# ScalarE counts the widest block of each search group by signs, the S5 matrix loads move to the SP queue, and a few scale steps to GpSimd

## The chip, the cores and the metric

The kernel runs on one core of a Trainium2 chip. The metric is the device time of one execution in microseconds (us). The engines are named as in the profile: PE is TensorE's matmul (PEld its weight load), DVE is VectorE, ACT is ScalarE, POOL is GpSimd, SP is SyncE, which here only issues DMAs. Each engine takes its instructions in a fixed order and waits at one that is not ready; a DMA is issued from an engine's queue, in the order of that engine.

## The reference

One layer over 1024 positions of width 1024. The input is normalised by its root mean square, scaled and shifted, and multiplied with one wide matrix; the columns of the product feed two mixers and their gates.

```
h = rms_norm(x, norm_g) * (1 + scale) + shift
xa, za, q, k, v, zb, qi, ki, wi, ga, gb = split(h @ w_in)
ya = gelu(s5_mixer(xa, ...)); ... ; ya = (ya * silu(za)) @ w_a_o
yb = dsa_mixer(q, k, v, qi, ki, wi);  yb = (yb * silu(zb)) @ w_b_o
merged = sigmoid(ga) * ya + sigmoid(gb) * yb
return x + gate * (merged @ w_out)
```

`s5_mixer` is a diagonal complex state space recurrence (32 groups of 16 channels, 64 states each). `dsa_mixer` is sparse attention: a small indexer gives each query a score for each earlier key, and the query attends only to the 256 keys of highest score. A final norm follows.

## The kernel before

Tiles are 128 positions, numbered 0 to 7; large products are split into a high and a low part and done as three matmuls of 128x512 (L137 to L139). The Tile framework's scheduler fixes each engine's order at build time from priorities and its own model of time; it also allocates buffers of one tag in the order in which the program names them.

**Norm.** `turn` works on pairs of tiles: ACT sums squares (L229), `rstd_of` (L85 to L96) turns the sums into scales with tiny DVE steps and one square root on ACT, DVE scales `x_sb` (L232), PE transposes (L236).

**Indexer scores** (L464 to L486) leave `score[i]` for tiles 2 to 7, of 128 x 128(i+1) numbers each.

**Search.** For each row the kernel looks for the value that 256 scores exceed, by 12 steps of bisection (L788 to L800). Tiles form two groups, (7, 5, 3) and (6, 4, 2). In each step DVE counts, for each of the three tiles of a group, the scores above the trial value `mid` (function `count`, L764 to L768: one pass with a running sum), ACT makes a sign of the three counts (`side`, L797), and ACT moves three `mid`s (L799). So there are 72 counts on DVE.

**Finalisation** (L801 to L818), tile by tile in the order 7, 5, 3, 6, 4, 2: one more count (`cj..._h`, written to the one buffer of tag "cj"), `j` (L812), the eight largest (L813), two tiny steps, a match and replace (L816), the mask (L817), and on ACT the additive `bias` of the attention (L818). The tile `j` has tag "cf" with two buffers; `gsum` (L722), a sum over eight loaded blocks `wg`, is named earlier under the same tag. Then DVE tests that all counts fit (`good`, `sound`, L822 to L824), PE sums the verdict over partitions (`flag_ps`, L826), and a branch (L830) takes a slow exact search if the test fails. PE's own row for the flag stands in its order after the matmuls of the gates and ahead of the attention's first (`l`, L891).

**S5** runs in eight blocks (q, L583 to L682). For a block GpSimd builds `mt` and `en` (L600 to L610), PE makes the kernel `k_ps` (L620), ACT copies it to `k` (L624), GpSimd adds a diagonal (L629), and eight small DMAs on ACT's queue spread it into the matrix `mk` (L632, two buffers). PE makes states (`s_ps`), ACT copies them (`sp`, L642), DVE rotates and scans them (L654 to L665) to `hs` (L670, L671), and PE adds the two products `u,mk` (L675) and `hs,en` (L677) to `y_ps`; ACT applies the activation (L680).

**Filling work.** Beside S5 PE runs the gate columns GA (eight blocks of 128 columns, 48 dense matmuls each, `gates`, L710 to L718), then GB 0 and 1 and ZB 0 to 3; each half block is evicted by ACT (L715), ZB's then also by DVE (L717). The other GB and ZA blocks fill the attention. The weights come by SP's queue (`load_w`, L108 to L115, two buffers), and are split by a cast on ACT and a subtraction on DVE (L77, L78).

Of the kernel before, what the change touches and what calls it, by code (L numbers as in the profile page):

```python
# [11 lines left out]
BF = mybir.dt.bfloat16  # L12
I32 = mybir.dt.int32
AF = mybir.ActivationFunctionType
OP = mybir.AluOpType
# [4 lines left out]
D = 1024  # L20
L = 1024
# [3 lines left out]
TOPK = 256  # L25
EPS = 1e-6
# [8 lines left out]
def tile_hybrid(ctx, tc, x, c, norm_g, w_mod, b_mod, w_in, a_re, a_im, b_re, b_im,  # L35
                c_re, c_im, d_skip, log_dt, w_glu, b_glu, w_a_o, w_b_o, w_out,
                final_g, out):
    nc = tc.nc
# [17 lines left out]
    def bank(name):  # L56
        return ps1.tile([128, 512], F32, name=name, tag="b1")
# [15 lines left out]
    def staged(name, dtype=F32, shape=(128, L)):  # L73
        return stage.tile(list(shape), dtype, name=name, tag="sg")
# [7 lines left out]
        tc.add_manual_dep(later.ins, earlier.ins.name, mybir.DependencyInfo(  # L82
            mybir.DependencyClass.NoSync, mybir.DependencyReason.DATA), reason="order")

    def rstd_of(t, n=1):  # L85
        a, b, y, r = (t[:, i * n:(i + 1) * n] for i in range(4))
        nc.vector.tensor_scalar(a, a, 1.0 / D, EPS, op0=OP.mult, op1=OP.add)
        nc.scalar.sqrt(b, a)
        nc.vector.reciprocal(y, b)
        if n == 1:  # L90
            nc.vector.scalar_tensor_tensor(b, y, a, y, op0=OP.mult, op1=OP.mult)
        else:
            nc.vector.tensor_mul(b, y, y)
            nc.vector.tensor_mul(b, b, a)
        nc.vector.tensor_scalar(b, b, -0.5, 1.5, op0=OP.mult, op1=OP.add)
        nc.vector.tensor_mul(r, y, b)  # L96
        return r
# [63 lines left out]
    T = 8  # L161
# [11 lines left out]
    with ExitStack() as st:  # L173
# [49 lines left out]
        def turn(half):  # L223

            for t2 in range(4 * half, 4 * half + 4, 2):
                stat = p0.tile([128, 8], F32, name=f"st{t2}", tag="st", bufs=4)
                for t in (t2, t2 + 1):
                    junk = p0.tile([128, D], BF, name=f"junk{t}", tag="junk", bufs=1)
                    nc.scalar.activation(junk, x_sb[t], AF.Square, accum_out=stat[:, t - t2:t - t2 + 1])  # L229
                rstd = rstd_of(stat, 2)  # L230
                for t in (t2, t2 + 1):
                    nc.vector.tensor_scalar_mul(x_sb[t], x_sb[t], rstd[:, t - t2:t - t2 + 1])  # L232
            for k in range(ND):
                ps = bank(f"xt{half}_{k}")
                for j in range(4):
                    nc.tensor.transpose(ps[:, 128 * j:128 * j + 128],  # L236
                                        x_sb[4 * half + j][:, 128 * k:128 * k + 128], ident)
                (nc.scalar.copy if k in ((0, 1, 3, 5, 7), (0, 1, 2, 3, 4, 5, 6, 7))[half] else nc.vector.tensor_copy)(
                    xT[k][:, 512 * half:512 * half + 512], ps)

        turn(0)
        h_hi, h_lo = parts(ND, "h")
        mp = bank("mod_ps")
# [29 lines left out]

        modulation(0)
        turn(1)
        modulation(1)
        qps = [[dense_bank(f"qi{m}_ps") if 2 * m + j < 3 else bank(f"qi{m}_ps") for j in range(2)]
               for m in range(3)]
        for dt in range(ND):
# [3 lines left out]
            scale, bias = ab[dt][:, 1:2], ab[dt][:, 0:1]  # L283

            for sl in [slice(512 * j, 512 * j + 512) for j in range(2)] if dt < 2 else [slice(0, L)]:
# [3 lines left out]
                for m in range(3):  # L289
                    a = slice(128 * m, 128 * m + 128)  # L290
                    for j in range(sl.start // 512, sl.stop // 512):
                        b = slice(512 * j, 512 * j + 512)
# [37 lines left out]
    score, bias = {}, {}  # L330
# [7 lines left out]
    sepool = search.enter_context(tc.tile_pool(name="sepool", bufs=1, side="right"))  # L338
    leads = []
    with ExitStack() as st:  # L340
# [23 lines left out]
        for e in range(2):  # L364
            a = slice(64 * e, 64 * e + 64)
# [98 lines left out]
        for i in groups[0] + groups[1]:  # L464
            w = 128 * (i + 1)
            for h in range(8):
                for o, n in chunks(w):
# [5 lines left out]
                    r = p1.tile([128, 512], F32, name=f"r{i}_{h}_{o}", tag="r", bufs=3)  # L473
# [4 lines left out]
                    else:  # L478
                        nc.vector.scalar_tensor_tensor(dst, r[:, :n], wi_t[:, i, h:h + 1], dst,  # L479
                                                       op0=OP.mult, op1=OP.add)  # L480
# [102 lines left out]
    for m in range(4):  # L583
# [3 lines left out]
        for half in range(2):  # L587
# [35 lines left out]
            ks_ = p2.tile([16, 4, T, 16], F32, name=f"k{q}", tag="kk", bufs=1)  # L623
# [5 lines left out]
            nc.gpsimd.tensor_add(ks_[:, :, 0], ks_[:, :, 0], dg)  # L629
            mk = mks[q % 2]  # L630
            for s in range(T):
                nc.scalar.dma_start(mk[s::8, :, s:], ks_[:, :, 0:T - s])  # L632

            ps = bank(f"s{q}_ps")
            for g in range(4):
# [10 lines left out]
            cj, sj = ct[:, jr], sn_t[:, jr]  # L646
# [3 lines left out]
            for ri in range(2):  # L650
# [11 lines left out]
                                         op0=OP.mult, op1=OP.add)  # L662
# [5 lines left out]
            for e in range(2):  # L668
                a = slice(64 * e, 64 * e + 64)
# [25 lines left out]
    t = staged("vraw")  # L695
# [27 lines left out]
    for kt in range(ND):  # L723
        t = staged(f"wg{kt}")
# [5 lines left out]
    b = staged("bgate")[0:1]  # L730
# [30 lines left out]
    def scr(name, dtype=F32, n=6):  # L761
        return sepool.tile([128, n], dtype, name=name)

    def count(src, at, op, dst, name, dtype=BF):  # L764
        w = src.shape[1]
        j = sepool.tile([128, L], dtype, name=name, tag="cj", bufs=1)[:, :w]
        nc.vector.tensor_scalar(j, src, at, None, op0=op, op1=OP.add, accum_out=dst)  # L767
        return j  # L768
# [4 lines left out]
    half = scr("half", n=STEPS + 2)  # L773
    for n in range(STEPS + 2):
        nc.gpsimd.memset(half[:, n:n + 1], 0.5 ** n)
    below, ranks = scr("below", n=1), scr("ranks", n=8)
    nc.gpsimd.memset(below, 0.5 - TOPK)
    for n in range(8):
        nc.gpsimd.memset(ranks[:, n:n + 1], float(TOPK - 1 - n))
    cgt = scr("cgt")  # L780
    best = sepool.tile([128, 12, 8], F32, name="best")
    step = sepool.tile([128, 6, STEPS + 2], F32, name="step")
    nc.vector.tensor_sub(most, most, least)
# [2 lines left out]
    mids, sides = ([[sepool.tile([128, 3], F32, name=f"{n}{g}", tag=f"{n}{g}", bufs=2)  # L786
                     for _ in range(STEPS + 1)] for g in range(2)] for n in ("mid", "side"))
    for g, tiles in enumerate(groups):  # L788
        for n, i in enumerate(tiles):
            nc.scalar.activation(mids[g][0][:, n:n + 1], least[:, i - 2:i - 1], AF.Identity,  # L790
                                 bias=step[:, i - 2, 1:2])
    for b in range(STEPS):
        for g, tiles in enumerate(groups):
            cnt = sepool.tile([128, 3], F32, name=f"cnt{g}_{b}", tag=f"cnt{g}", bufs=2)
            for n, i in enumerate(tiles):
                count(score[i], mids[g][b][:, n:n + 1], OP.is_gt, cnt[:, n:n + 1], f"cj{i}_{b}")
            nc.scalar.activation(sides[g][b], cnt, AF.Sign, bias=below)  # L797
            for n, i in enumerate(tiles):
                nc.scalar.activation(mids[g][b + 1][:, n:n + 1], sides[g][b][:, n:n + 1], AF.Identity,  # L799
                                     scale=step[:, i - 2, b + 2:b + 3], bias=mids[g][b][:, n:n + 1])  # L800
    for g, tiles in enumerate(groups):  # L801
        for n, i in enumerate(tiles):
            e = slice(i - 2, i - 1)
            nc.scalar.activation(sides[g][STEPS][:, n:n + 1], mids[g][STEPS][:, n:n + 1], AF.Identity,
                                 bias=step[:, i - 2, STEPS + 1:])
# [24 lines left out]
    with tc.If(found < 6 * 128):  # L830
# [4 lines left out]
        thr, d, cnt, need = scr("thr", I32), scr("d", I32), scr("cntb"), scr("need")  # L835
# [196 lines left out]
    for k, (m, pieces) in enumerate(steps):  # L1032
# [8 lines left out]
        t = wpool.tile([128, D], F32, name=f"wo{k}", tag="wraw")  # L1041
# [7 lines left out]
    for t in range(NT):  # L1049
        tok = slice(128 * t, 128 * t + 128)  # L1050
        xr, y = xy[:, t % 2], xy[:, 2 + t % 2]
        nc.sync.dma_start(xr, x[tok])
        stat = const.tile([128, 8], F32, name=f"fs{t}", tag="fs", bufs=2)

        pieces = [(0, 512), (512, 512)] if t < NT - 1 else [(0, 512), (512, 256), (768, 256)]
        for n, (o, w) in enumerate(pieces):
            sl = slice(o, o + w)
            ps = pso.tile([128, 512], F32, name=f"o{t}_ps", tag="o")
            for kt in range(ND):
                three(ps[:, :w], m_hi[kt][:, tok], m_lo[kt][:, tok], wo_h[kt][:, sl], wo_l[kt][:, sl],  # L1060
                      kt == 0, kt == ND - 1)
            nc.vector.tensor_mul(y[:, sl], ps[:, :w], gate[:, sl])
            nc.vector.tensor_add(y[:, sl], y[:, sl], xr[:, sl])
            nc.scalar.activation(xr[:, sl], y[:, sl], AF.Square, accum_out=stat[:, 4 + n:5 + n])
        nc.vector.tensor_add(stat[:, 0:1], stat[:, 4:5], stat[:, 5:6])
        if t < NT - 1:
            rstd = rstd_of(stat)
            nc.vector.scalar_tensor_tensor(y, y, rstd, fg, op0=OP.mult, op1=OP.mult)
            nc.sync.dma_start(out[tok], y)
        else:  # L1070
            a, b = slice(0, 512), slice(512, 1024)
            nc.gpsimd.tensor_mul(y[:, a], y[:, a], fg[:, a])
            nc.vector.tensor_add(stat[:, 0:1], stat[:, 0:1], stat[:, 6:7])
            rstd = rstd_of(stat)
            nc.scalar.activation(y[:, a], y[:, a], AF.Copy, scale=rstd)
            nc.scalar.dma_start(out[tok, a], y[:, a])
            nc.vector.scalar_tensor_tensor(y[:, b], y[:, b], rstd, fg[:, b], op0=OP.mult, op1=OP.mult)
            nc.sync.dma_start(out[tok, b], y[:, b])
# [28 lines left out]
```

## Time and profile before

| | |
|---|---|
| time, median of 3 runs | 905.83 us (901.27 to 908.48) |
| the profiled execution | 904.93 us, its span 903.2 us |
| busy over the span | PE 854.9 us (95%), DVE 655.7 (73%), ACT 406.5 (45%), POOL 138.4 (15%) |
| mean granted clock of TensorE | 0.981 of full speed |
| matmuls | 4105 |
| the 72 counts of the search on DVE | 67.6 us, 939 ns each |

A busy row adds the durations of an engine's instructions. A timeline row gives the start, the length, the engine, the line and the tile, and in brackets how long the engine stood idle before it and what released it. A wait row sums those idle times by instruction and releaser. The granted clock is a share of full speed. The mean time of an instruction includes its fixed part, so that of two that follow each other the second can start before the first's end.

### The profile page before, as it was taken

The page shows a single profiled execution, that of the slowest core. Times are in us where ns is not written, and L with a number is a line of the kernel's source. Part 1 is how long each engine was busy: PE and PEld are TensorE (multiplying, and loading weights), DVE is VectorE, ACT ScalarE, POOL GpSimd, SP SyncE. Part 2 cuts the span into 40 slices and gives each one's busy share as a digit, 9 for nine tenths or more (in the row PEclk, how much of TensorE's full clock was granted, in tenths as well). Part 3 has the DMA queues.
Part 4 walks back from the last instruction along what each step waited for, and adds up shares of the span by engine and source line. Part 5 has one row for each costly group of instructions (what it writes and reads, how often), then busy time and mean ns, then how long its engine had stood idle before and what let it go on. Part 6 is the DMA issues. An engine that isn't in the chain of part 4 may idle for free. (4 is left out here: it accounts for less than half of the span.)

```text
span 903.2 us, 12003 instructions
## 1 busy us (share of the span) xinstructions
PE 854.9 (95%) x4105; PEld 704.1 (78%) x4105; DVE 655.7 (73%) x1381; ACT 406.5 (45%) x803; POOL 138.4 (15%) x244
## 2 busy tenths in 40 slices
PE   4999999998889998999989999999999999999996
PEld 4887788876678876878868888887888888777885
DVE  5674898488999895588236776678987776856753
ACT  7552576344446443322235555448564443432311
POOL 0000100069455944000000000000000000221000
PEclk9799999999899999999999999999999999999999
DMA  9925611363443423473334232235224232644431
GB/s 330 319 66 126 154 49 46 66 178 91 122 113 124 113 78 99 124 279 94 117 107 128 88 97 73 70 106 166 68 64 135 71 94 81 216 143 143 151 129 48
DMA packets 124228, 109.86 MB, mean 122 GB/s; under 512 B 20922, under 2 KB 108034, under 8 KB 124164
## 3 DMA queue, kind: packets, MB, share of 16 engines
q1 hardware_dynamic: 96306, 77.20, 28.3%
q10 hardware_dynamic: 27858, 31.87, 12.2%
q8 instruction: 32, 0.52, 0.3%
q14 instruction: 32, 0.26, 0.1%
HBM read 76.41 MB, written 26.22 MB: 114 GB/s over the span
## 5 line engine op out<-in xcount | busy, mean ns | idle before, releaser
L78 POOL TENSOR_TENSOR wo_l<-wo,wo_h 128x1024 fp32r<-128x1024 f32 x5 | 12.2, 2444 | 451.7 <-ACT wo_h L77 423.2
L767 DVE TENSOR_SCALAR_CACHE_REDUCE cj<-score,mid 128x1024 bf16<-128x1024 f32 (+2 forms) x72 | 67.6, 939 | 14.6 <-ACT mid L790 9.1
L894 DVE CUSTOM_DVE_ANT_0 S<-l,bias 128x384 f32<-128x384 f32 (+5 forms) x96 | 52.4, 554 | 27.1 <-PE l L891 18.5
L905 ACT ACTIVATE S<-S,stt 128x128 f32<-128x128 f32 (+7 forms) x64 | 49.1, 770 | 37.3 <-DVE stt L902 37.1
L77 ACT CAST ph<-pt 128x512 fp32r<-128x512 f32 x72 | 41.3, 585 | 43.2 <-PE pt L916 38.1
L78 DVE TENSOR_TENSOR pl<-pt,ph 128x512 fp32r<-128x512 f32 x72 | 48.9, 687 | 9.2 <-ACT ph L77 8.8
L137 PE MATMUL gb_ps<-h_hi,gb_wh 128*128 128x512 f32 x128 | 52.0, 406 | 2.0 <-ACT gbs L715 2.0
L891 PE MATMUL l<-k_s,qt 128*128 128x384 f32 (+5 forms) x192 | 49.9, 347 | 3.4 <-issue 2.3
L138 PE MATMUL gb_ps<-h_lo,gb_wh 128*128 128x512 f32 x128 | 52.3, 408 | 0.0
L139 PE MATMUL gb_ps<-h_hi,gb_wl 128*128 128x512 f32 x128 | 51.7, 404 | 0.0
L138 PE MATMUL o_ps<-wo_l,m_hi 128*128 128x512 f32 (+1 forms) x136 | 51.2, 378 | 0.0
L139 PE MATMUL o_ps<-wo_h,m_lo 128*128 128x512 f32 (+1 forms) x136 | 51.0, 378 | 0.1
L137 PE MATMUL ga_ps<-h_hi,ga_wh 128*128 128x512 f32 x128 | 50.8, 397 | 0.0
L139 PE MATMUL ga_ps<-h_hi,ga_wl 128*128 128x512 f32 x128 | 50.7, 396 | 0.0
L138 PE MATMUL ga_ps<-h_lo,ga_wh 128*128 128x512 f32 x128 | 50.2, 392 | 0.0
L474 ACT ACTIVATE r<-s 128x512 f32<-128x512 f32 (+3 forms) x80 | 39.8, 525 | 22.8 <-PE s L470 16.8
L137 PE MATMUL o_ps<-wo_h,m_hi 128*128 128x512 f32 (+1 forms) x136 | 49.4, 377 | 0.1
L479 DVE SCALAR_TENSOR_TENSOR score<-r,wi_t,score 128x512 f32<-128x512 f32 (+3 forms) x70 | 42.1, 653 | 7.5 <-ACT r L474 6.6
L916 PE MATMUL pt<-ident,S 128*128 128x128 f32 x288 | 46.3, 273 | 0.4 <-DVE S L909 0.4
L916 PEld LDWEIGHTS pt<-ident,S 128*128 128x128 f32 x288 | 36.6, 140 | 11.3 <-DVE S L909 1.0
L470 PE MATMUL s<-ki_s,qi_s 128*128 128x384 f32 (+3 forms) x160 | 42.2, 356 | 1.4 <-DVE wi_t L463 0.9
L891 PEld LDWEIGHTS l<-k_s,qt 128*128 128x128 f32 x192 | 33.9, 189 | 9.7 <-issue 2.4
(402 smaller groups left out, 2402.5 us busy)
## 6 DMA issues: line engine op xcount, KB each, us to landing
wm<-in_w_mod_dram SPq DMA_DIRECT2D x16, 512.0 KB, 6.3
x_sb<-in_x_dram SPq DMA_DIRECT2D x8, 512.0 KB, 5.5
ga_w<-in_w_in_dram SPq DMA_DIRECT2D x8, 512.0 KB, 4.1
gad<-gas ACTq DMA_DIRECT2D x8, 512.0 KB, 2.6
gb_w<-in_w_in_dram SPq DMA_DIRECT2D x8, 512.0 KB, 4.4
wg<-in_w_mod_dram SPq DMA_DIRECT2D x8, 512.0 KB, 5.2
gbd<-gbs ACTq DMA_DIRECT2D x8, 512.0 KB, 3.2
qt<-qd SPq DMA_DIRECT2D x8, 512.0 KB, 3.9
```

The costliest lines, as they stand in the source:

```text
L77: (hi_eng or nc.scalar.copy)(hi, src)
L78: (lo_eng or nc.vector).tensor_sub(lo, src, f32(hi))
L137: paced(nc.tensor.matmul(ps, wh, rh, start=first, stop=False))
L138: paced(nc.tensor.matmul(ps, wh, rl, start=False, stop=False))
L139: mm = nc.tensor.matmul(ps, wl, rh, start=False, stop=last)
L470: mm = nc.tensor.matmul(ps[:, :n], qs[:, h, 128 * i:128 * i + 128], ks[:, e, o:o + n], start=e == 0, stop=e == 1)
L479: nc.vector.scalar_tensor_tensor(dst, r[:, :n], wi_t[:, i, h:h + 1], dst, op0=OP.mult, op1=OP.add)
L767: nc.vector.tensor_scalar(j, src, at, None, op0=op, op1=OP.add, accum_out=dst)
L891: mm = nc.tensor.matmul(ps[:, :n], qt[:, 4 * e2 + 2 * j + g], ks[:, e, o:o + n], start=e == 0, stop=e == 1)
L894: nc.vector.tensor_tensor_reduce(out=S[:, o:o + n], in0=ps[:, :n], in1=bias[i][:, o:o + n], scale=1.0, scalar=NEG, op0=OP.add, op1=OP.max, ...
L905: nc.scalar.activation(S2[j], S2[j], AF.Exp, scale=0.125, bias=nm[:, j:j + 1], accum_out=sm[:, j:j + 1])
L916: mm = nc.tensor.transpose(ps[:, 128 * j:128 * j + 128], Ss[i, g, j][:, 128 * kb:128 * kb + 128], ident)
```

## The change

There are three edits. First, in each of the 12 steps the widest tile of each group (7 and 6) is counted on ACT: a Sign of `mid - score` with a running sum, its elementwise result thrown into `ca`, a scratch tile of tag "cf". The sum is the number of scores below less the number above, so `side` of that tile is made by an instruction of its own with another bias (`signs`) and scale -1, and the one `side` of three counts becomes two. DVE keeps 48 of the 72 counts. Second, the 64 loads of `mk` are issued from SP and no longer from ACT. Third, for the pairs of the second half of the positions five of `rstd_of`'s steps run on GpSimd.

```diff
-    def rstd_of(t, n=1):
+    def rstd_of(t, n=1, eng=None):
+        if eng is not None:
+            eng.tensor_scalar(a, a, 1.0 / D, EPS, op0=OP.mult, op1=OP.add)
+            nc.scalar.sqrt(b, a)
+            nc.vector.reciprocal(y, b)
+            eng.tensor_mul(b, y, y)
+            eng.tensor_mul(b, b, a)
+            eng.tensor_scalar(b, b, -0.5, 1.5, op0=OP.mult, op1=OP.add)
+            eng.tensor_mul(r, y, b)
+            return r
...
-                rstd = rstd_of(stat, 2)
+                rstd = rstd_of(stat, 2, nc.gpsimd if half else None)
...
-                nc.scalar.dma_start(mk[s::8, :, s:], ks_[:, :, 0:T - s])
+                nc.sync.dma_start(mk[s::8, :, s:], ks_[:, :, 0:T - s])
...
+    signs = {}
+    ca = sepool.tile([128, L], BF, name="ca", tag="cf", bufs=2)
+    for g, i in ((0, 7), (1, 6)):
+        signs[i] = scr(f"signs{i}", n=1)
+        nc.gpsimd.memset(signs[i], 128.0 * (i + 1) + 1 - 2 * TOPK)
...
-                count(score[i], mids[g][b][:, n:n + 1], OP.is_gt, cnt[:, n:n + 1], f"cj{i}_{b}")
-            nc.scalar.activation(sides[g][b], cnt, AF.Sign, bias=below)
+                if n:
+                    count(score[i], mids[g][b][:, n:n + 1], OP.is_gt, cnt[:, n:n + 1], f"cj{i}_{b}")
+                else:
+                    nc.scalar.activation(ca[:, :128 * (i + 1)], score[i], AF.Sign, scale=-1.0, bias=mids[g][b][:, 0:1],
+                                         accum_out=cnt[:, 0:1])
+            nc.scalar.activation(sides[g][b][:, 0:1], cnt[:, 0:1], AF.Sign, scale=-1.0, bias=signs[tiles[0]])
+            nc.scalar.activation(sides[g][b][:, 1:3], cnt[:, 1:3], AF.Sign, bias=below)
```

How the change stands in the engines' orders is shown at three places. The line numbers of the changed kernel are 10 higher from `load_w` on and 21 higher behind the search's steps.

**ACT, the start of the search.** Before, the first step's `side` stands in ACT's order ahead of S5's first copies. Now the first Sign (L815, the line that writes `ca` and `cnt_0`) comes behind nearly all of S5 and the eviction of the first half of GA's last block (the second `gas` here).

```order
L725 ACTIVATE gas_3387<-ga_ps 128x512
L652 COPY sp_2636<-s_ps 64x256 x4
L728 DMA gad<-gas_3387 128x1024
L725 ACTIVATE gas_3447<-ga_ps 128x512
L815 ACTIVATE ca,cnt_0_4024<-score_717,mid_3966 128x1024
L77 CAST v_s<-v_ps 128x8x64
L817 ACTIVATE side_3992<-cnt_0_4024,signs_3958 128x1
L815 ACTIVATE ca,cnt_0_4035<-score_715,mid_3979 128x896
L820 ACTIVATE mid_3967<-side_3992,mid_3966,step 128x1
```

All 24 Signs stand from this place to the next one; before, the 24 `side` rows were spread over S5 and all stood ahead of this place.

**ACT, the end of the search**, in the changed kernel; `zbs_3840` is the block ZB 3, the last of PE's dense work ahead of the flag, and L825 the last move of tile 7's trial value, from which the finalisation counts.

```order
L815 ACTIVATE ca,cnt_11_4277<-score_715,mid_3990 128x896
L818 ACTIVATE side_4003<-cnt_11_4266,below 128x2
L820 ACTIVATE mid_3990<-side_4015,mid_3989,step 128x1 x2
L820 ACTIVATE mid_3978<-side_4003,mid_3977,step 128x1
L817 ACTIVATE side_4016<-cnt_11_4277,signs_3960 128x1
L728 DMA zbd<-zbs_3778 128x1024
L820 ACTIVATE mid_3978<-side_4003,mid_3977,step 128x1 x2
L725 ACTIVATE zbs_3840<-zb_ps 128x512
L825 ACTIVATE side_4004<-mid_3978,step 128x1
```

Before, L825's forerunner (L804) stood within S5; now it stands behind the eviction of ZB 3's first half.

**DVE, the finalisation.** Before, the count `cj_h` of tile 7 stood in the middle of S5 and `j` right behind the first piece of `gsum`, with the rest of both interleaved from there on:

```order
L692 TENSOR_SCALAR bg<-bg 128x4
L78 TENSOR_TENSOR v_s<-v_ps,v_s 128x8x64
L727 TENSOR_SCALAR gsum<-wg_3508,sc 128x1024
L812 SCALAR_TENSOR_TENSOR j_4286<-cj_h,score_717 128x1024
L78 TENSOR_TENSOR gb_wl<-gb_w,gb_wh 128x1024
L729 SCALAR_TENSOR_TENSOR gsum<-wg_3511,sc,gsum 128x1024
```

In the changed kernel the whole of it comes behind the eviction of ZB 3 (the first row here), and the second step's counts come where `j` was:

```order
L727 SCALAR_TENSOR_TENSOR zbs_3840<-zbs_3840,zb_ps 128x512
L777 TENSOR_SCALAR cj_h,cgt<-score_717,side_4004 128x1024
L833 SCALAR_TENSOR_TENSOR j_4291<-cj_h,score_717 128x1024
L835 TENSOR_SCALAR best<-ranks,cgt 128x8
L834 MAX best<-j_4291 128x8
L836 SCALAR_TENSOR_TENSOR best<-best 128x8
L78 TENSOR_TENSOR gb_wl<-gb_w,gb_wh 128x1024
L752 TENSOR_TENSOR bgate<-bgate,gate_3904 1x512
L837 MATCH_REPLACE j_4291<-best,j_4291 128x1024
L727 SCALAR_TENSOR_TENSOR zbs_3840<-zbs_3840,zb_ps 128x512
L752 TENSOR_TENSOR bgate<-bgate,gate_3907 1x512
```

From here to `sound` DVE's order holds the finalisation alone. On SP the eight loads of a block's `mk` now stand between the loads of GA's weights, where eight `ga_w` stood in a row before. On PE the order of the dense work, the flag and the attention is what it was.

## Rows read from the trace of the kernel before

**Rows 1.** What PE waited for, whole span (engine, line, releaser: us in total, times, longest).

```profile
PE y_ps L677 <- DVE hs L671: 7.8, 6, 1.9
PE xt L236 <- DVE x_sb L232: 7.2, 4, 5.3
PE y_ps L675 <- DMA mk<-k: 5.8, 3, 3.6
...
PE k_ps L620 <- POOL en L610: 2.3, 1, 2.3
```

**Rows 2.** Busy us (and instructions) of each engine by stretch, PE's granted clock, DMA share, GB/s.

```profile
225.00:250.00 25.00, 21.37 (x96) 17.85 (x95) 24.64 (x34) 9.03 (x24) 12.70 (x16) 0.86 0.46 119
250.00:275.00 25.00, 22.11 (x104) 18.26 (x103) 22.33 (x40) 13.80 (x31) 11.18 (x13) 0.93 0.47 124
...
381.00:452.00 71.00, 68.97 (x302) 56.00 (x301) 46.79 (x76) 18.10 (x27) 0.00 (x0) 0.98 0.51 163
```

**Rows 3.** Timeline of PE in S5 (start, length, instruction, idle before and releaser).

```profile
241.54 0.77 PE L675 MATMUL y_ps<-u,mk 128*128 128x128 f32 x2 [3.63 <-DMA mk<-k]
...
259.76 0.49 PE L677 MATMUL y_ps<-hs,en 128*128 128x128 f32 x2 [1.95 <-DVE hs L671]
...
261.42 0.80 PE L677 MATMUL y_ps<-hs,en 128*128 128x128 f32 x2 [0.94 <-DVE hs L671]
...
342.55 0.46 PE L677 MATMUL y_ps<-hs,en 128*128 128x128 f32 x2 [1.58 <-DVE hs L671]
```

**Rows 4.** Timeline of PE from the first GB matmul to the flag.

```profile
380.09 0.39 PE L137 MATMUL gb_ps<-h_hi,gb_wh 128*128 128x512 f32 x1
...
451.02 1.88 PE L741 MATMUL gate<-gsum,ones 128*1 128x512 f32 x4
452.73 0.19 PE L826 MATMUL flag_ps<-ones,sound 128*1 128x1 f32 x2
```

**Rows 5.** Timeline of DVE, the finalisation of the search.

```profile
327.06 1.27 DVE L767 TENSOR_SCALAR_CACHE_REDUCE cj_h<-score,side 128x1024 bf16<-128x1024 f32 x1
...
381.01 1.22 DVE L812 SCALAR_TENSOR_TENSOR j<-cj_h,score 128x1024 f32<-128x1024 bf16 x1
...
404.62 0.75 DVE L767 TENSOR_SCALAR_CACHE_REDUCE cj_h<-score,side 128x512 bf16<-128x512 f32 x1 [0.91 <-ACT bias L818]
...
429.05 0.08 DVE L824 DVE_READ_ACCUMULATOR good<-cgt,good 128x1 f32 x1
```

**Rows 6.** DVE by form: two passes over the widest tile in the finalisation (busy, mean ns).

```profile
L813 DVE MAX8 best<-j 128x8 f32<-128x1024 f32 x1 | 1.2, 1220 | 0.0
...
L817 DVE SCALAR_TENSOR_TENSOR cj_h<-j,cj_h 128x1024 bf16<-128x1024 f32 x1 | 1.2, 1215 | 0.0
```

**Rows 7.** ACT by form: wide instructions with a sum, evictions, casts (busy, mean ns).

```profile
L715 ACT ACTIVATE gbs<-gb_ps 128x512 f32<-128x512 f32 x16 | 9.3, 590 | 7.8 <-DVE gsum L729 4.7 <-PE gb_ps L139 2.1 <-DVE best L815 1.0
...
L905 ACT ACTIVATE S<-S,stt 128x1024 f32<-128x1024 f32 x8 | 9.1, 1144 | 2.5 <-DVE stt L902 2.4
...
L77 ACT CAST gb_wh<-gb_w 128x1024 fp32r<-128x1024 f32 x8 | 8.4, 1048 | 17.1 <-PE zb_ps L138 9.3 <-PE gb_ps L138 5.1 <-PE ga_ps L138 2.7
...
L905 ACT ACTIVATE S<-S,stt 128x896 f32<-128x896 f32 x8 | 8.3, 1038 | 2.4 <-DVE stt L902 2.4
```

**Rows 8.** Timeline of ACT, one step of the search late in S5.

```profile
308.72 0.30 ACT L797 ACTIVATE side<-cnt,below 128x3 f32<-128x3 f32 x1
309.05 0.95 ACT L799 ACTIVATE mid<-side,mid,step 128x1 f32<-128x1 f32 x3
```

**Rows 9.** Timeline of ACT, the last evictions of GA.

```profile
373.61 0.60 ACT L715 ACTIVATE gas<-ga_ps 128x512 f32<-128x512 f32 x1 [0.57 <-PE ga_ps L139]
```

**Rows 10.** Timeline of ACT, the second block's `k` and its loads (ACTq: its issues).

```profile
232.00 0.58 ACT L624 COPY k<-k_ps 16x512 f32<-16x512 f32 x1
...
235.03 5.11 ACTq L632 DMA_DIRECT2D mk<-k  x8
```

**Rows 11.** Timeline of DVE beside busy GpSimd: a split of a weight block.

```profile
224.55 6.53 DVE L78 TENSOR_TENSOR kv_wl<-kv_w,kv_wh 128x1024 fp32r<-128x1024 f32 x1
```

## The prediction

> **What bounds the kernel now.** I read the busy times first (the table of the section on the profile): PE works 854.9 of 903.2 us, so the time is PE's work and its gaps, and a change pays only where it moves a gap of PE. The list of PE's waits says which gaps there are: most are 7.8 us for DVE's `hs`, 7.2 us for the scaled `x_sb` at the start, 5.8 us for `mk`, and 2.3 us for GpSimd's `en` [rows 1]. Three of these four belong to S5. The table by stretch shows what else they cost: from 225 to 250 us PE is busy 21.37 of 25 us and its clock falls to 0.86, from 250 to 275 to 0.93, and DVE is busy for 24.64 of the 25 us in the first of them [rows 2]. So S5 is where the edits can win. The second place to read is the end of the search. Before, PE reaches the flag at 452.73 us and waits for nothing there [rows 4], because DVE had the verdict `sound` at 429.05 [rows 5]: the search has 23.7 us of slack and costs PE nothing. What the change does to that slack decides the case.
>
> **The search, what is removed and added.** DVE loses 24 counts, about 1.2 us each; this alone is at most 29 us of an engine that isn't the bound. ACT gets 24 Signs with a sum and 24 more `side`s. The trace has no Sign of that width; nearest are ACT's wide instructions with a sum and a pointer for the bias, 1.144 us at 1024 and 1.038 us at 896 columns [rows 7]; I take these. A `side` and the first `mid` that follows it are 0.33 us apart, three `mid`s take 0.95 us [rows 8]. A step of both groups is then 1.14 + 1.04 + 4 x 0.33 + 2 x 0.95 = 5.4 us of ACT if each waits for the one before, and about 4.7 us if the two groups overlap (the Signs some 0.1 us less each, a `side` 0.25, a `mid` 0.28). Twelve steps are 57 to 65 us.
>
> **Where the search now stands** matters more than its price. The scratch `ca` has the tag of `gsum`, which the program names first, and the order of the changed kernel puts the first Sign behind the eviction of the first half of GA's last block. Before, that eviction ran from 373.61 to 374.2 [rows 9], 6 us ahead of the first GB matmul at 380.09 [rows 4]. Call the latter T. The whole search, which before was over at 327.06, when tile 7's last count `cj_h` began [rows 5], now begins at T - 6. Between the first Sign and the end of the steps ACT has in its order two casts of GB's and four of ZB's weights (1.05 us each), two half-size instructions, and eleven evictions (0.59 us each) [rows 7]: 14 us by durations, 12 where they overlap. ACT thus ends the steps at T - 6 + 69 to 79, that is T + 63 to T + 73. PE bounds it too: the last move of tile 7 (L825) stands behind the eviction of ZB 3's first half, and PE's dense work, 2 + 4 blocks of 48 matmuls, took from T to 451.02 [rows 4], 0.246 us each, and the second half of ZB 3 is 24 of them, 5.9 us; so the eviction came at T + 65. I take T + 67, and the finalisation at T + 67.5.
>
> **The finalisation** was before mixed with other DVE work and hidden under PE's GB and ZB. Now it stands alone at the end. A tile of 1024 columns takes five passes, the count of 1.27 and four of about 1.22 us [rows 5, 6], 6.15 us in all, and some 0.65 us for three tiny steps and the hand-overs (an estimate). The six tiles have 4224 columns, so 4224/1024 x 6.15 + 6 x 0.65 = 29.3 us, less 0.9 for the last tile's two passes behind `sound`: 28.4. Between tiles DVE waits for ACT's `bias`, since the count of the next tile writes the same buffer: 0.91 us at one place [rows 5], about 0.9 at each of five, 4.6. The changed order adds the split of a GB block (1.2), two steps on the gate (0.6 each) and one eviction (0.6). The sum is 28.4 + 4.6 + 3.0 = 36.0 us. `sound` comes at T + 103.5; the flag stood at T + 72.6 (452.73 less 380.09). All of PE's attention stands behind the flag in its order, and nothing of the dense work left is ahead of it, so PE idles for the difference: **31 us later**. Even with the steps free of charge `sound` would come at T + 65 + 36, 29 us later than the flag did; with the steps at their dearest at T + 73 + 36, 37 us. So 28 to 38.
>
> **S5 and its matrix loads.** DVE loses nearly all counts there, not only the two widest: of 72 it keeps four. ACT no longer issues the loads. Before, `k` of the second block was done at 232.58, the issue of its `mk` began at 235.03 and took 5.11 us [rows 10], and PE waited 3.63 us at 241.54 for the last of them [rows 3]. On SP the eight issues remain one after the other; what goes is the start behind other work of ACT, at most 2.4 us here. I take 3.5 us of the 5.8 for `mk` back (bounds 0 and 5.8). Of the 7.8 for `hs`, 2.9 (1.95 at 259.76 and 0.94 at 261.42) lie where the counts were; the others, as at 342.55 [rows 3], came after the search had ended and stay. The wait for `en` is GpSimd's and stays. The clock: at 0.86 and 0.93 over two stretches of 25 us PE lost 25 x 0.14 + 25 x 0.07 = 5.2 us [rows 2]; with about half the gaps gone I take 2.6 back. Sum **9 us** (bounds 0 and 23: all of S5's gaps, 15.9 with the one for `en`, and its clock, 7 with a third stretch as dear as the second).
>
> **The weights on SP.** The loads of GA 1 to 7 now stand behind blocks' `mk`, and SP waits at an `mk` until GpSimd has finished `k`. Behind it wait only weights that are needed some tens of us later (a GA block is 48 matmuls, and S5's own work between them); I price it at nothing, its cover being that lead; if it is gone, the price is an `mk`'s issue and a weight's landing, 5 to 10 us in all.
>
> **The start.** Of 7.2 us waiting for `x_sb`, 5.3 are the first pair's [rows 1], which is not of the second half. Five steps move from a busy DVE to an idle GpSimd in two pairs; 0 to 1.9 us, I take **1**.
>
> The sum, on the profiled run's 904.93 us: 904.93 + 31 - 9 - 1 = **926 us**. The median of the runs shown, 905.83, is 0.9 above that run, well inside the range.
>
> **The rivals.**
> *S5 pays it all back.* DVE free of counts lets `hs` come early in all eight blocks, the gaps of S5 and its clock go, 23 us, the start gives 2, and the tail is at its floor of 29: 904.93 + 29 - 25 = 909 us. This is within 1% of before. For it speaks that DVE was busy for 24.64 of 25 us in the worst stretch; the Trainium skill gives the same reason (Perfetto Trace Analysis, Optimizing Scalar/DVE Operations): where VectorE is saturated, handing work to ScalarE may make sense. Against it, the waits for `hs` after 327 us came without a count near. To end at 905 S5 would have to give back what the tail costs, so the point is 29 us, more than its gaps hold.
> *S5 gives nothing.* The split of a weight block took 6.53 us at 224.55 beside GpSimd [rows 11]; a pass of two inputs of that size takes 1.22 [rows 5]. GpSimd's work is all still there, and if it is what makes `hs` late, the counts' leaving does nothing: 904.93 + 31 = 936. The Trainium skill says that GpSimd shares its SBUF interfaces with VectorE and contends with its instructions of two SBUF inputs (GPSIMD Engine Reference, Key points). By that page the split's length is contention, which the row bears out; that all of S5's gaps are, no row shows.
> *The steps run slower.* A step goes ACT, DVE, ACT twice, in order, between evictions; if waits add 0.4 to 1 us to each of twelve, and ACT's late evictions hold PE, the tail is 36 to 43 us: 931 to 940.
> *It is faster.* One mechanism: the Signs start long before T (the counts of step 0 on DVE still stand early), so that the finalisation has its slack again. It decides where the search begins 31 us earlier, at T - 37; then only S5's gain is left, 895 us. The order of ACT, which is fixed at build time, speaks against it.
> *The check fails.* If Sign's sum miscounts, the slow search of 31 counts for six tiles runs: about 31 x 6 x 0.94 = 175 us, 1100 in all.
>
> **How the numbers follow.** The forecast with its neighbours (918 to 933) 0.53, S5 gives nothing 0.17, slower steps 0.15, S5 pays all 0.09, faster 0.04, the check fails 0.02. The predicted time is the likeliest, 926. The range from 911 to 940 leaves out the faster case, part of the paying one, the failed check and the dear end. About 1% is what a measurement of this kernel can tell from no change, so 897 and 915 are the bounds: faster 0.03, within 0.09, slower 0.88.
>
> **What would show it.** In the profile after: one gap of some 28 to 38 us on PE right at the flag or the first `l`, with the finalisation ending last; the first Sign within a few us of GB's first matmul; 4.7 to 5.4 us from one step to the next; PE's waits for `mk` below 3 us and for `hs` near 5; the wait for `en` unchanged; the DVE split beside GpSimd as long as before. A gap below 20 us at the flag, or S5's gaps gone altogether, would make this wrong.

## The result, and the profile after

The changed kernel takes 926.27 us (median; 924.94 to 928.51), the kernel before 903.66 in the runs beside it. The ratio is 1.0244, with a 95% interval from 1.0215 to 1.0274: slower. The profiled execution has a span of 926.7 us; PE is busy for 850.7 us of it, 4.2 less than before, and that is now 92%.

What PE waited for after the change (columns as in [rows 1]):

```profile
PE flag_ps L847 <- DVE good L845: 31.2, 1, 31.2
...
PE gb_ps L147 <- ACT gbs L725: 5.0, 1, 5.0
PE ga_ps L149 <- DVE ga_wl L78: 3.7, 1, 3.7
PE y_ps L687 <- DVE hs L681: 3.3, 2, 1.8
PE y_ps L685 <- DMA mk<-k: 2.6, 1, 2.6
...
PE mt_ps L623 <- POOL mt L612: 1.4, 1, 1.4
PE k_ps L630 <- POOL en L620: 1.4, 1, 1.4
```

One wait is new and larger than all the others shown here together: 31.2 us at the flag, for `good`. The waits for `hs` and `mk` went from 7.8 and 5.8 to 3.3 and 2.6, and that for `en` from 2.3 to 1.4; but a wait of 3.7 us for the split of a GA weight block has come in, one of 5.0 at a GB eviction (2.0 before), and that for `mt` rose from 0.5 to 1.4. PE's timeline at the places of [rows 4]:

```profile
374.68 0.39 PE L147 MATMUL gb_ps<-h_hi,gb_wh 128*128 128x512 f32 x1
...
446.97 1.88 PE L751 MATMUL gate<-gsum,ones 128*1 128x512 f32 x4
480.01 0.19 PE L847 MATMUL flag_ps<-ones,sound 128*1 128x1 f32 x2 [31.17 <-DVE good L845]
480.68 1.09 PE L912 MATMUL l<-k_s,qt 128*128 128x128 f32 x4 [0.48 <-DVE rows_ok L849]
```

The first GB matmul (T) is 5.4 us earlier than before (380.09). The flag is 105.3 us behind T, where it was 72.6. The next matmuls of the attention, `l`, follow it by 0.7 us, before by 2.5. Added up, `l` is 25.4 us later than before, and the span 23.5 us longer.

What ACT did between T - 8 and the end of the search (L815 is the Sign with its sum, L825 the last move of tile 7's trial value):

```profile
367.10 1.14 ACT L815 ACTIVATE ca<-score,mid 128x1024 bf16<-128x1024 f32 x1
...
434.56 1.15 ACT L815 ACTIVATE ca<-score,mid 128x1024 bf16<-128x1024 f32 x1
...
441.63 0.60 ACT L725 ACTIVATE zbs<-zb_ps 128x512 f32<-128x512 f32 x1 [0.97 <-PE zb_ps L149]
442.13 0.28 ACT L825 ACTIVATE side<-mid,step 128x1 f32<-128x1 f32 x1
```

The first Sign starts at T - 7.6. From the first to the twelfth Sign of tile 7 are 67.5 us, 6.13 us a step; in 8.1 of these 67.5 us ACT stood idle. The last move stands right behind the eviction of ZB 3's first half, for which ACT waited 0.97 us for PE. And DVE, at the places of [rows 5]:

```profile
442.87 1.27 DVE L777 TENSOR_SCALAR_CACHE_REDUCE cj_h<-score,side 128x1024 bf16<-128x1024 f32 x1
...
454.63 1.01 DVE L777 TENSOR_SCALAR_CACHE_REDUCE cj_h<-score,side 128x768 bf16<-128x768 f32 x1 [1.37 <-ACT bias L839]
...
479.87 0.08 DVE L845 DVE_READ_ACCUMULATOR good<-cgt,good 128x1 f32 x1
```

The finalisation starts at T + 68.2 and has its verdict 37.1 us later. Until it is through PE has nothing to do. The table by stretch (columns as in [rows 2]) shows this, and what S5 looks like:

```profile
225.00:250.00 25.00, 21.21 (x109) 17.23 (x108) 23.18 (x28) 9.70 (x18) 12.97 (x16) 0.98 0.43 122
300.00:325.00 25.00, 21.33 (x96) 17.16 (x95) 24.74 (x17) 6.41 (x13) 14.92 (x21) 0.86 0.30 89
452.00:478.00 26.00, 0.00 (x0) 0.00 (x0) 20.66 (x39) 5.27 (x6) 0.00 (x0) 0.50 0.06 24
478.00:483.00 5.00, 2.51 (x10) 2.14 (x11) 3.08 (x14) 1.81 (x2) 0.00 (x0) 0.50 0.01 2
483.00:487.00 4.00, 4.00 (x16) 3.23 (x15) 0.99 (x7) 0.88 (x4) 0.00 (x0) 0.74 0.23 55
```

From 452 to 478 us PE runs no instruction at all, while DVE is busy for 20.66 of 26 us. After it the granted clock is at 0.50 from 478 to 483, the lower of TensorE's two levels (1.2 of 2.4 GHz), 0.74 in the next 4 us, and then full. In S5 the low stretch has moved: 225 to 250 is now at 0.98 (0.86 before), and 300 to 325 at 0.86 (1.00 before), with DVE busy for 24.74 of 25 us in only 17 instructions. Two of these are the splits of GA weight blocks. The tile view (shortest, median and longest, in ns):

```profile
L78 DVE TENSOR_TENSOR ga_wl<-ga_w,ga_wh x2: 1211/9026/16840, 298.9 to 315.6; 128x1024 fp32r<-128x1024 f32 x2
```

and the timeline of GpSimd and PE there:

```profile
313.39 1.25 POOL L585 TENSOR_TENSOR sn_t<-sn_t,rv 128x512 f32<-128x512 f32 x1
...
315.78 0.79 PE L149 MATMUL ga_ps<-h_hi,ga_wl 128*128 128x512 f32 x1 [3.67 <-DVE ga_wl L78]
```

One split took 1.2 us and the other 16.84. GpSimd had worked without a break since before 298.9; it paused at 314.64, and the split ended a microsecond later, when PE's wait of 3.67 us for it ended too.

### The profile page after: what moved, and what is told of

It reads as the page before. It is cut to its first block, busy times and chain, and to the rows that moved or that the text cites. A ratio compares the mean times of both kernels' runs of the same rounds, so it can differ in the third digit from the quotient of the medians.

```text
span 926.7 us, 12037 instructions
## 1 busy us (share of the span) xinstructions
PE 850.7 (92%) x4105; PEld 701.4 (76%) x4105; DVE 646.1 (70%) x1323; ACT 436.2 (47%) x875; POOL 137.2 (15%) x256
## 4 chain that ended last, share of the span: by engine, by line
PE 57%; DVE 13%; DMA 3%; ACT 2%; issue 2%; POOL 1%; SPq 0%; ACTq 0%; DVEq 0%; POOLq 0%
PE l L912 4%; PE pt L937 3%; PE gb_ps L147 3%; PE gb_ps L148 3%; PE o_ps L149 3%; PE gb_ps L149 3%; PE o_ps L148 3%; PE o_ps L147 3%; PE ga_ps L149 2%; PE ga_ps L147 2%; PE ga_ps L148 2%; DVE ga_wl L78 2%; PE pv L957 2%; PE pv L956 2%; PE ao_ps L149 2%
## 5 line engine op out<-in xcount | busy, mean ns | idle before, releaser
L777 DVE TENSOR_SCALAR_CACHE_REDUCE cj<-score,mid 128x768 bf16<-128x768 f32 (+3 forms) x48 | 38.9, 811 | 8.4 <-ACT mid L820 4.9
L937 PEld LDWEIGHTS pt<-ident,S 128*128 128x128 f32 x288 | 36.6, 140 | 10.3
```

Source lines behind the costliest of these rows:

```text
L937: mm = nc.tensor.transpose(ps[:, 128 * j:128 * j + 128], Ss[i, g, j][:, 128 * kb:128 * kb + 128], ident)
```

## The experiments

The theory was that the search is late because `ca` needs a buffer of `gsum`'s tag; the rival, that counting on ACT is too slow for its place. "Before" in the ratios is always the kernel before, timed beside the experiment: 903.85 us beside the first four, 904.64 beside the others. So two experiments are best compared by their ratios. At run time the changed kernel's first Sign does not wait for `gsum`: it starts at 367.10, and DVE's first write of `gsum` at 369.67. If the theory holds, the tag acts at build time, through the order.

**`e1_ca_first`: the changed kernel, with `ca` written ahead of `gsum`.** (Naming it earlier alone left the order as it was; its first use is what counts.)

```diff
+    ca = sepool.tile([128, L], BF, name="ca", tag="cf", bufs=2)
+    nc.gpsimd.memset(ca[:, 0:1], 0.0)
     gsum = sepool.tile([128, D], F32, name="gsum", tag="cf", bufs=2)
...
-    ca = sepool.tile([128, L], BF, name="ca", tag="cf", bufs=2)
```

> The changed kernel with one addition: ca is named and first written (one column set to zero by GpSimd) ahead of gsum, so that it gets its buffer of tag cf first; all three edits stay. Theory A (the search is late because ca waits behind gsum for a buffer): the Signs start in S5, the finalisation is hidden again, PE's wait at the flag (31.2 us) goes, and the time is 926.3 - 31 + 0 to 6 for Signs that now stand between S5's copies on ACT: 895 to 902 us. Rival B (the counting on ACT is itself too slow for the place): the wait at the flag stays above 10 us and the time above 910.

Measured: 900.07 us, ratio 0.995 (0.9928 to 0.9972). One memset of 128 numbers takes back the whole loss and leaves a kernel that is 0.5% faster than before. Its timeline:

```profile
320.39 1.25 POOL L585 TENSOR_TENSOR sn_t<-sn_t,rv 128x512 f32<-128x512 f32 x1
...
448.32 1.88 PE L753 MATMUL gate<-gsum,ones 128*1 128x512 f32 x4
450.04 0.19 PE L848 MATMUL flag_ps<-ones,sound 128*1 128x1 f32 x2
452.56 0.63 PE L913 MATMUL l<-k_s,qt 128*128 128x128 f32 x4 [2.33 <-issue]
```

The flag follows the gate without a wait, as it did before, and `l` is at 452.56 (before 455.25). All 24 Signs are still on ACT, and they are early, as Theory A has it: the tile view of `ca` gives their shortest, median and longest time in ns and their first and last start.

```profile
L816 ACT ACTIVATE ca<-score,mid x24: 1027/1090/1153, 181.8 to 281.0; 128x1024 bf16<-128x1024 f32 x12, 128x896 bf16<-128x896 f32 x12
```

Two of PE's waits, and the split:

```profile
PE ga_ps L149 <- DVE ga_wl L78: 7.2, 1, 7.2
...
PE y_ps L685 <- DMA mk<-k: 4.5, 1, 4.5
```

```profile
L78 DVE TENSOR_TENSOR ga_wl<-ga_w,ga_wh x2: 1210/10764/20318, 302.4 to 322.7; 128x1024 fp32r<-128x1024 f32 x2
```

The split beside GpSimd is longer still, 20.3 us, and ends at 322.7, again a microsecond after GpSimd's last instruction (320.39 + 1.25); PE now waits 7.2 us for it.

**`e2_tag_only`: the kernel before, all counts on DVE, but the two widest of a step write their discarded result into a tile of tag "cf".**

```diff
+    ca = sepool.tile([128, L], BF, name="ca", tag="cf", bufs=2)
...
+                if n:
                     count(score[i], mids[g][b][:, n:n + 1], OP.is_gt, cnt[:, n:n + 1], f"cj{i}_{b}")
+                else:
+                    nc.vector.tensor_scalar(ca[:, :128 * (i + 1)], score[i], mids[g][b][:, 0:1], None, op0=OP.is_gt,
+                                            op1=OP.add, accum_out=cnt[:, 0:1])
```

> The kernel before with no Sign: all 72 counts stay on DVE, and only the two widest of a step write their discarded result into ca, a tile of tag cf, instead of the tile of tag cj. Theory A: the search starts behind gsum and runs beside GB and ZB; 12 steps at 6.5 us on DVE with 25 us of other DVE work end at about T + 95 (T: first GB matmul), the finalisation 36 us later, the flag some 58 us later than before: 955 to 970 us. Rival B: no ACT work is added, so 905 us as before.

Measured: 946.68 us, ratio 1.0478 (1.0448 to 1.0509), with this wait:

```profile
PE flag_ps L831 <- DVE good L829: 49.9, 1, 49.9
```

No instruction has changed its engine and none is added; only the tag of a scratch tile is another, and the kernel is 43 us slower. The 58 us expected at the flag were 47 (it stands at 501.81, 119.6 behind this run's T of 382.18): the order is the theory's, the estimate of DVE's work beside GB and ZB was too high. With the counts on DVE the late search costs more than with a third of them on ACT; for the place that they were put in, the Signs were a help (930.38 us with them and no other edit, in the next experiment).

**`e4_signs_only`: the changed kernel, with the loads back on ACT and the scale steps back on DVE.**

```diff
-                rstd = rstd_of(stat, 2, nc.gpsimd if half else None)
+                rstd = rstd_of(stat, 2)
...
-                nc.sync.dma_start(mk[s::8, :, s:], ks_[:, :, 0:T - s])
+                nc.scalar.dma_start(mk[s::8, :, s:], ks_[:, :, 0:T - s])
```

> The changed kernel with the mk loads back on ACT and the scale steps back on DVE: only the signs. By the sum of the prediction with the parts as measured (flag 32.7 us later against the first GB matmul, some 4 us won back behind the flag), 928 to 934 us: 928 if what S5 won comes from the counts that left DVE, 934 if it came from the mk loads.

Measured: 930.38 us, ratio 1.0299 (1.0267 to 1.0330).

```profile
PE flag_ps L847 <- DVE good L845: 33.9, 1, 33.9
```

It lies between the two cases named. The wait at the flag makes all of the loss, and the other two edits together are worth some 4 us in the changed kernel (926.27 us with them); the intervals of the two ratios just overlap.

**`e3_mk_only`: the kernel before, with the loads on SP.**

```diff
-                nc.scalar.dma_start(mk[s::8, :, s:], ks_[:, :, 0:T - s])
+                nc.sync.dma_start(mk[s::8, :, s:], ks_[:, :, 0:T - s])
```

> The kernel before with the mk loads on SP alone. If the loads' start behind ACT's other work is what PE waits for, PE's wait for mk falls from 5.8 to 2 to 3 us and the time by 2 to 4: 900 to 902 against 903.7. If the eight issues one after the other are what counts, the wait stays near 5 and the time within 1 us. If SP's queue holds weights back, PE waits for weights and the time rises by 5 to 10.

Measured: 910.75 us, ratio 1.0090 (1.0059 to 1.0122): none of the three. PE's waits:

```profile
PE y_ps L677 <- DVE hs L671: 11.7, 9, 3.6
...
PE y_ps L675 <- DMA mk<-k: 4.4, 2, 2.3
```

The wait for `mk` fell, by less than hoped (5.8 to 4.4), PE waits for no weight, and the wait for `hs` grew from 7.8 to 11.7. What ACT waits for, of this kernel and then of the one before, says where the time went:

```profile
ACT side L797 <- DVE cj L767: 38.9, 16, 6.8
```

```profile
ACT side L797 <- DVE cj L767: 21.5, 9, 5.0
...
ACT sp L642 <- DMA mk<-k: 12.4, 3, 4.8
```

ACT no longer waits for `mk`, and instead stands 38.9 us at `side`, for counts of DVE (21.5 before). At one place all of it can be followed, in the timeline:

```profile
307.44 1.28 DVE L767 TENSOR_SCALAR_CACHE_REDUCE cj<-score,mid 128x1024 bf16<-128x1024 f32 x1
...
311.94 7.33 DVE L78 TENSOR_TENSOR ga_wl<-ga_w,ga_wh 128x1024 fp32r<-128x1024 f32 x1
...
317.58 0.61 POOL L571 TENSOR_TENSOR rv<-sn_t,wrot 128x256 f32<-128x256 f32 x1
...
320.76 0.30 ACT L797 ACTIVATE side<-cnt,below 128x3 f32<-128x3 f32 x1 [6.79 <-DVE cj L767]
...
322.97 0.57 ACT L616 COPY mi<-mt_ps 128x512 f32<-128x512 f32 x1
...
323.59 0.82 PE L636 MATMUL s_ps<-u,mi 128*128 128x128 f32 x5 [4.39 <-ACT mi L616]
```

A split of two inputs, started at 311.94, is held until GpSimd pauses (317.58 + 0.61) and ends at 319.27. The counts behind it are late; `side` waits 6.79 us for them, and behind `side`, in ACT's order, stands `mi`, for which PE waits 4.39 us. So here ACT, freed of the issues, ran into the next wait, and in the changed order a split stood where GpSimd was busy; a second one, at 327.69, took 8.16 us. How much of the 7 us comes from these places is not shown: the profiled run took 908.19 us, 3.3 more than the profiled run of before and less than half of the loss.

**`e5_ca_first_rot`: `e1_ca_first`, with S5's second rotation on DVE.**

```diff
+        eng = nc.vector if j0 else nc.gpsimd
         for e in range(7):
...
-            nc.gpsimd.tensor_mul(u, st_[:, :, 0:k], wi_)
+            eng.tensor_mul(u, st_[:, :, 0:k], wi_)
```

and so for the other five lines of the loop.

> The kernel with ca first (900.1 us) with one more edit: S5's second rotation (36 small products and sums of two inputs) is made by DVE and no longer by GpSimd. Theory: there a split of a GA weight block on DVE took some 20 us (1.2 elsewhere) because GpSimd's rotation ran beside it without a break, and PE waited 7.2 us for it; without GpSimd's work the splits take 1.2 us, the wait goes and with it some 3 us of lowered clock, less up to 5 for 12 us of rotation on DVE: 891 to 896 us. Rival: the split is long for another reason (a late wait, the weight's landing, ACT's cast): it stays above 5 us, and the time is 900 or, with DVE's added work, up to 908.

Measured: 901.56 us, ratio 0.9965 (0.9944 to 0.9987). The splits of GA's weights, by form:

```profile
L78 DVE TENSOR_TENSOR ga_wl<-ga_w,ga_wh 128x1024 fp32r<-128x1024 f32 x8 | 10.3, 1291 | 3.6 <-ACT yg L691 3.6
```

All eight together take 10.3 us, 1.29 each; in the changed kernel they took 25.4, and in `e1_ca_first` 29.4. PE's wait for them is gone. So GpSimd's work is what held them. The time didn't follow: the interval overlaps that of `e1_ca_first`. T is 1.7 us earlier than there (377.40 against 379.10), and PE waits elsewhere:

```profile
PE y_ps L686 <- DMA mk<-k: 4.9, 2, 4.3
PE y_ps L688 <- DVE hs L682: 3.3, 3, 1.7
...
PE s_ps L647 <- ACT mi L627: 2.4, 1, 2.4
```

**`e8_before_rot`: the kernel before, with the same edit.**

> The kernel before with S5's second rotation on DVE alone. There the split beside that rotation took 4.5 us and cost PE little; DVE is busy with the counts. If GpSimd's rotation is what holds DVE's instructions of two inputs, that split takes 1.2 us and the waits for hs at 333 and 342 to 345 (4.9 us) shrink, while 12 us more on a busy DVE delay the counts, which have 23.7 us of slack: 898 to 904. If DVE's load is what counts, 906 to 912.

Measured: 905.86 us, ratio 0.9999 (0.9980 to 1.0018).

```profile
L78 DVE TENSOR_TENSOR ga_wl<-ga_w,ga_wh 128x1024 fp32r<-128x1024 f32 x8 | 11.2, 1406 | 5.1 <-ACT ga_wh L77 5.1
```

```profile
PE y_ps L678 <- DVE hs L672: 9.3, 6, 3.7
...
PE y_ps L676 <- DMA mk<-k: 4.6, 4, 2.9
```

The splits are short here too, and the time is the same; PE's wait for `hs` is 9.3 us instead of 7.8. The splits take 3.0 us less than before (11.2 against 14.2), and the rotation takes 18.2 us of DVE, not the 12 expected. That the one pays for the other is likely, but not shown.

**`e6_ca_first_nomk` and `e7_ca_first_nors`: `e1_ca_first`, with the loads back on ACT, and with the scale steps back on DVE** (each with its half of the diff of `e4_signs_only`).

> The kernel with ca first (900.1 us), with the mk loads back on ACT. The loads alone on SP made the kernel before slower (910.8 against 903.9), by waits for hs and mi that the mk loads have no part in. If SP is the worse queue for them in itself, this is 893 to 898. If with the Signs on ACT the loads are better off SP's way, this is 902 to 906: ACT's issues (5.1 us a block) now stand between Signs.

> The kernel with ca first (900.1 us), with the scale steps back on DVE. By the prediction's third part they are worth 0 to 1.9 us: 900 to 902. If their place at the start shifts the order of what follows, more than 3 us either way.

Measured: 904.82 us, ratio 1.0000 (0.9984 to 1.0017), and 903.43 us, ratio 0.9978 (0.9960 to 0.9995). The 0.5% that `e1_ca_first` gains over the kernel before goes with the loads: the Signs and the scale steps without them gain nothing. With the loads on ACT, PE waits 6.9 us for them instead of 4.5, and 6.2 us at a GB eviction:

```profile
PE y_ps L685 <- DMA mk<-k: 6.9, 3, 3.9
PE gb_ps L147 <- ACT gbs L725: 6.2, 1, 6.2
```

The same edit that costs 0.9% in the kernel before is worth 0.5% once ACT has the Signs, and has them early; which wait makes the difference is not shown. The scale steps are worth about 0.3%, within what these runs can tell from nothing.

## Why the prediction was right, by its steps

**The place of the search: right, and shown.** The sum hung on the order and not on the price of a Sign. `e2_tag_only` shows that the tag alone makes the kernel slower, and `e1_ca_first` that the Signs cost nothing where the tag lets them start in time. The prediction named the cause, but gave as its reason, like the section on the kernel before, that `gsum` is named first. What counts is the first use: with `ca` merely named ahead of `gsum` the order stayed, and with one write ahead of it the search came early. Nor did it say how cheap the way out was.

**The steps: right.** 6.13 us a step, less 13 to 14 us of casts and evictions over twelve, is 5.0 us, between the 4.7 and 5.4 given; the Signs took 1.14 and 1.03 us. Two errors offset each other in this: 0.7 us of the step are ACT's idle time (8.1 us over eleven), so its work was some 4.3 us, less than the 4.7 of the sum. And the sign given in the last paragraph, 4.7 to 5.4 us from one step to the next, left out the casts and evictions that the sum had; it read 6.13. They start at T - 7.6 (T - 6 forecast), the finalisation at T + 68.2 (T + 67.5).

**The finalisation: right.** 37.1 us against 36.0. The five waits for `bias` sum to 4.8 us (4.6 forecast), though not at 0.9 each: they go with the width of the tile just finished, 0.70 us at 512 columns and 1.02 at 896, and 1.37 at 1024, where ACT had the issue of the gate's row ahead of `bias`. What the sum had not was 1.04 us that DVE stood for a cast. (The floor and the top of this term were rounded up: 65 + 36 - 72.6 is 28.4 and not 29, and 73 + 36 - 72.6 is 36.4 and not 37.) The flag: 32.7 us later behind T, 31 forecast.

**Behind the flag: missed, in the kernel's favour.** The sum carried the delay to the end unchanged. But 1.85 us of it came back at once: PE's idle time ahead of `l`, 2.33 us before, for which the profile shows no releaser, is 0.48 us behind the long wait. Another 1.9 us came back in the attention. Of these 1.35 are idle time of PE (13.1 us from `l` to the end before, 11.8 after): PE's first waits there, for DVE's `stt` and `S`, 1.5 us together, are gone behind the long wait. Nor did the sum price the clock behind the gap, about 2.3 us (2.51 us busy at 0.50 and 4.0 at 0.74 granted); but before there were two stretches of 3 us there at 0.64 and 0.79, with PE busy for 2.75 and 2.74 us, 1.6 us.

**S5: the step that was mis-sized.** Forecast 9 us; PE gained 5.4 us until T, of which 1.4 were won ahead of S5 (it reached its first wait for `mt` at 194.26 and not 195.65). That leaves 4.0. The terms: for `mk` 3.2 (3.5 forecast), for `hs` 4.5 (2.9 forecast, more of it came back than was thought), the clock nothing (2.6 forecast: by the prediction's own way of counting 7.0 us lost before and 6.8 after, at another place), and against them new waits of 3.7 for the split and 0.4 for `mi`; 0.9 won on `en` went on `mt`. These waits sum to 3.6; the other 0.4 is busy time. The rival that S5 gives nothing rested on [rows 11], GpSimd holding DVE's instructions of two inputs, and it was half right: where the counts left, a split moved under GpSimd's rotation and was held for 16.84 us. The split of that row itself took 11.54 us, at 216.28, against the sign that it would be as long as before. The prediction took that row for a price that stays as it is; it is a price that depends on what GpSimd does at that moment, and a change of order moves it.

**The loads on SP: right in size in this kernel, wrong as a rule.** The prediction costed them against the waits of before, as if the order around them stayed. Alone they cost 7 us; with the Signs early they give 4 to 5, and with the Signs late some 4 together with the scale steps. No weight came late, as forecast: PE waits for none, and ACT's casts of `ga_w` waited for PE and for no DMA.

**The start: right in size, its cause not shown.** PE was 1.4 us earlier at S5 (1 forecast, the bound 1.9), but its waits for `x_sb` sum to 7.3 us, as before, and `e7_ca_first_nors` can't tell the scale steps from nothing.

The sums then cancel: 32.7 - 5.4 - 3.8 = 23.5 us of span, where 31 - 9 - 1 = 21 was forecast. The time lies near the forecast because a tail that was 1.7 us longer and an S5 that gave 5 us less stand against 3.8 us behind the flag that were in no term. The mechanism is the one forecast. That 926 and 926.27 agree within 0.3 us is luck: the terms' errors offset each other, and the forecast stood on a run 1.3 us above the 903.66 measured beside the change.

## What to carry to other kernels

A scratch tile is not free because it is never read: its buffer's tag ties it to the tiles that are used ahead of it under the same tag, and so can move a whole chain of work in the order. Read where the first instruction of a chain stands in the order before costing what it does, and when a chain that was hidden becomes late, add up all that hangs on its end. An edit that is worth something beside another edit may cost something alone, so cost it in the order that it will have.

## What was not expected of the hardware

On DVE an instruction of two inputs made almost no headway while GpSimd worked on tensors without a pause. A split of 128x1024 takes 1.22 us with GpSimd idle (at 243.00 before). It took 6.53 before at 224.55 [rows 11], and 7.33, 11.54, 16.84 and 20.3 us in the runs above, and in each of these cases ended 1.0 to 1.1 us after GpSimd's last instruction of the stretch: it is not slowed by a factor, it stands until GpSimd lets go. A count of one tensor input beside the same work took 1.28 us as ever (at 307.44 in `e3_mk_only`). The Trainium skill (GPSIMD Engine Reference, Key points) states that GpSimd contends with VectorE's instructions of two SBUF inputs. These runs agree, and `e5_ca_first_rot` shows that with the rotation off GpSimd the splits are short again; a split beside the first rotation, which GpSimd kept, took 6.87 us there (at 209.56).

It holds the other way round too, and it does not always take an idle GpSimd to end it. From the kernel before:

```profile
321.91 4.53 DVE L78 TENSOR_TENSOR ga_wl<-ga_w,ga_wh 128x1024 fp32r<-128x1024 f32 x1
...
325.32 1.27 POOL L626 TENSOR_TENSOR dg<-dsk,ident 16x64 f32<-16x64 f32 x1
```

This split ended at 326.44, 1.1 us after GpSimd's instruction ahead of `dg` (325.35), and now `dg`, 0.28 us elsewhere (at 236.69), took 1.27. What let the split in between the two is not shown.

Nor are two tensor inputs the whole condition. In `e6_ca_first_nomk` an instruction of 128x8 numbers, with one tensor input and a scalar for each partition, was held as long:

```profile
315.79 10.37 DVE L836 TENSOR_SCALAR best<-ranks,cgt 128x8 f32<-128x8 f32 x1
```

Its five other instances there took 0.22 to 0.23 us. It ended at 326.16, and GpSimd's stretch at 326.12. Why the counts, which also have one tensor input and such a scalar, are not held, no run here shows.
